# A decoder kernel on one core: a third seven-product unit pair in the early parts of both down projections, and two in the last part

## The chip, the core and the metric

The kernel runs on one core of one Trainium2 chip. Times are microseconds (us) of that core on the device. A kernel's time is the median of several runs; its profile is of one execution by itself. In profile rows PE is TensorE (PEld its weight loads), DVE is VectorE, ACT is ScalarE, POOL is GpSimd, SP is SyncE, which issues the weight loads.

## The reference

Two decoder layers over 256 tokens of width 2048. The first layer mixes tokens with gated linear attention, the second with attention that has a forget gate; both also attend with 4 heads into 256 memory tokens, and the heads' outputs go through one output projection (`wo`). Behind each mixer stands the feed-forward network that the change is about:

```python
def conv_ffn(h, w_up, conv_w, conv_b, w_down):
    u = causal_dwconv(h @ w_up, conv_w, conv_b)     # width 3, 2 x 5632 columns
    a, val = split_cols(u, [FFN_HIDDEN, FFN_HIDDEN])
    return (jax.nn.silu(a) * val) @ w_down          # 5632 -> 2048

# per layer
    x = x + mixer(...)
    h = rmsnorm(x, norm_ffn[i])
    x = x + conv_ffn(h, ffn_w_up[i], ffn_conv_w[i], ffn_conv_b[i], ffn_w_down[i])
# at the end
    return rmsnorm(x, norm_final)
```

Everything is float32 in and out.

## The kernel before

**Products.** TensorE's fast 32-bit type keeps fewer bits than float32, so each operand is held as a high part and a low part (the rounded value and the rest), and a product is three matmuls: high x high, low x high, high x low. Activations lie as chunks of 128 features (`A0`, `A1`, ... and `B0`, ...), each with its two parts for 256 tokens, made by `split` (ScalarE the high part, L464; VectorE the low part, L465).

**Units.** A weight panel is 512 output columns. It comes in units of two chunks (128 x 1024 values, 512 KB). SP loads a unit as `raw` (4 buffers), ScalarE rounds it to `whi` (L207), VectorE subtracts to `wlo` (L216); 3 buffers each. A unit gives 12 matmuls of 128x512: two chunks, two halves of the tokens, three products. Sums build up in PSUM tiles `acc` (4 banks). `proj_tm` does one panel, `proj_two` two panels at once with the last `late` units of both held back.

**Seven products.** `proj_seven` does two panels at once. For a pair of units (same chunks, panels f and f+1) that stands in `forms`, it takes the four blocks (two chunks, two panels) against two token halves as a 2x2 by 2x2 block product with 7 block products rather than 8: 21 matmuls, not 24. VectorE makes weight sums `t13` and `t24` (four 128x512 operations, L335 to L338), ScalarE and VectorE the high and low parts of raw unit 0, of half of raw unit 1 (`vhi`, `vlo`), of `t13` and of `t24`; the activations need sums too (`summed`: four `sf` operations of 128x128, then the parts of `forms`, 128x512). Four block products go to banks of their own (`ps_t`, `ps_s` twice, `ps_o`) and are added to `x` by `more` (s16, s167).

**Feed-forward network.** The hidden width is 44 chunks in three parts of 16, 16 and 12. For each part the "up" panels are computed, scaled, transposed through DRAM, and two chunks at a time go through `taken` (convolution, Silu, multiply, `split`), which is put behind a number of units by `later` and `passed`. Then the part's down projection adds its four panels f = 0 to 3 to `x`. Parts 0 and 1 have 8 units per panel; both panel pairs use `proj_seven` with unit pairs u = 3 and 5 (`SEVEN`). The last part has 6 units per panel: panels 0 and 1 by `proj_two`, 2 and 3 by `proj_tm`. In the last part of layer 1 the final norm's gain `gf` (1 MB) is loaded, and each panel is multiplied by it.

**Order.** A scheduler puts each engine's instructions in a fixed order, by priority (`tc.high_priority`; weights get `AHEAD`); an engine runs its instructions in that order.

Of the kernel before, what the change touches and what calls it, by code (L numbers as in the profile page):

```python
# [136 lines left out]
def _trunk(ctx: ExitStack, tc: tile.TileContext, xt, xtok, memt, wp, wgu, gns, gfin, cnv, par, msk, out):  # L137
# [128 lines left out]
                    for b in range(2):  # L266
                        evacs[i](b, acc[i][b][:, : units[i][0][2]])

    def proj_seven(keys, src, forms, evacs, pool, more):

        units = [where[k] for k in keys]
        count = len(units[0])
        base = min(min(u[1]) for u in units[0])
        acc = [[pacc.tile([P, 512], F32, name="acc", tag="acc") for _ in range(2)] for _ in keys]
        m1, m5, m6, m7 = (work(t, n) for t, n in (("t", 1), ("s", 2), ("o", 1), ("s", 2)))
        begun, calls = set(), {}

        def form(a, x, hi, lo, c):
            s = slice(c * 512, (c + 1) * 512)
            out = []  # L280
            for xs, w in ((x[0], hi), (x[1], hi), (x[0], lo)):
                out.append((a, xs, w[:, s]))
            return out

        def emit(groups):
            todo = [g[n] for n in range(2) for g in groups] + [g[2] for g in groups]
            for a, x, w in todo:
                k = id(a)
                calls[k] -= 1
                TE.matmul(a, x, w, start=k not in begun, stop=calls[k] == 0)  # L290
# [12 lines left out]
        def token(kc, b):  # L303
            return [src[kc - base][:, i, b * P : (b + 1) * P] for i in range(2)]

        def halves(raw, w):
            if w == NUNIT:
                hi, lo = (wpool.tile([P, w], F32R, name=n, tag=n, bufs=3) for n in ("whi", "wlo"))
            else:
                hi, lo = (pool.tile([P, w], F32R, name=n, tag=n) for n in ("vhi", "vlo"))  # L310
            casts.append(S.activation(hi, raw, AF.Copy))
            V.tensor_tensor(lo, raw, hi.bitcast(F32), ALU.subtract)
            return hi, lo

        def load(unit):
            off, kcs, n = unit
            raw = wpool.tile([P, NUNIT], F32, name="raw", tag="raw", bufs=4)
            loads.append(nc.sync.dma_start(raw, wp[off : off + P * NUNIT].rearrange("(p n) -> p n", p=P)))
            return raw

        for u in range(count):
            k0, k1 = units[0][u][1]
            if u not in forms:
                for i in range(2):
                    hi, lo = split_unit(units[i][u])
                    emit([form(acc[i][b], token(kc, b), hi, lo, c) for b in range(2) for c, kc in enumerate((k0, k1))])
                    if u == count - 1:
                        for b in range(2):
                            evacs[i](b, acc[i][b])
                continue  # L330
            s = forms[u]
            with tc.high_priority(offset=AHEAD + 40):
                r0, r1 = (load(units[i][u]) for i in range(2))
                t13, t24 = (pool.tile([P, 2, 512], F32, name=n, tag=n) for n in ("t13", "t24"))
                V.tensor_tensor(t13[:, 0, :], r1[:, :512], r0[:, :512], ALU.subtract)  # L335
                V.tensor_tensor(t13[:, 1, :], r1[:, 512:], r1[:, :512], ALU.subtract)
                V.tensor_tensor(t24[:, 0, :], r1[:, 512:], t13[:, 0, :], ALU.subtract)
# [614 lines left out]
    def add_seven(key, src, forms, pool):  # L952
        for f in (0, 2):
            def more(m1, m5, m6, m7, x0=x[f], x1=x[f + 1]):
                u, w = (pool.tile([P, 512], F32, name=n, tag=n) for n in ("s16", "s167"))
                V.tensor_tensor(x0[:, 0, :], x0[:, 0, :], m1, ALU.add)
                S.activation(u, m1, AF.Copy)
                V.tensor_tensor(u, u, m6, ALU.add)
                V.tensor_tensor(x1[:, 0, :], x1[:, 0, :], u, ALU.add)
                V.tensor_tensor(w, u, m7, ALU.add)  # L960
                V.tensor_tensor(x0[:, 1, :], x0[:, 1, :], w, ALU.add)
                V.tensor_tensor(x1[:, 1, :], x1[:, 1, :], w, ALU.add)
                V.tensor_tensor(x1, x1, m5.unsqueeze(1).to_broadcast([P, 2, 512]), ALU.add)

            proj_seven([(*key, g) for g in (f, f + 1)], src, forms, [add_panel(g) for g in (f, f + 1)], pool, more)

    def ffn(l, nx, h, m, then, ending=None):
        with tc.tile_pool(name=f"ffn{l}", bufs=1) as fp, ExitStack() as ends:
            sums = ends.enter_context(ExitStack())
            sp = sums.enter_context(tc.tile_pool(name=f"sums{l}", bufs=1))  # L970
            cw = fp.tile([P, 4 * 88], F32, name="cw")
# [2 lines left out]
            for u in us:  # L974
                nc.gpsimd.memset(u[:, :, :2], 0.0)
            turn = [0]
            forms = {u: sp.tile([P, 2, 4, P], F32R, name=f"forms{u}") for u in SEVEN}
            held = []

            def form(t):  # L980
                return lambda i: [t[:, h, i, :] for h in range(2)]

            def taken(j, base, u, i):
# [11 lines left out]
                S.activation(cv[0], cv[0], AF.Silu)  # L995
                V.tensor_tensor(cv[1], cv[0], cv[1], ALU.mult)
                split(m, j + i - base, cv[1])
                if base < PARTS[-1][0] and (j - base) // 2 in forms:
                    held.append(cv[1])
                    if i:  # L1000
                        summed(forms[(j - base) // 2])

            def summed(form):
                h0, h1 = (natural(h) for h in held)
# [24 lines left out]

                return evac  # L1030

            spare = None
            for p, (lo, hi) in enumerate(PARTS):
                if p == len(PARTS) - 1:
                    sums.close()
                    if ending is not None:
                        then, spare = ending(ends)
                js = list(range(lo, hi, 2))
                if not p:
                    proj_two([("up", l, j) for j in js[:2]], h, [panel(js[0], lo), panel(js[1], lo, 2)], 2)  # L1040
                    js = js[2:]
                for j in js:
                    proj_tm(("up", l, j), h, panel(j, lo))
                if p < len(PARTS) - 1:
# [35 lines left out]

    fin = StreamNorm()

    def ending(ends):
        op = ends.enter_context(tc.tile_pool(name="store", bufs=1))
        gf = op.tile([P, D], F32, name="gf")
        nc.sync.dma_start(gf, gfin.to_broadcast([P, D]))
        y = op.tile([P, 2, 512], F32, name="y")
        junk = op.tile([P, 1], F32, name="junk")

        def then(f, b):  # L1090
            fin.add(f, b)
            if f == 0 and b == 0:
                S.activation(junk, fin.sums[:, 0, 0:1], AF.Sqrt)
            dst = y if f == 3 else x[f]
            V.tensor_tensor(dst[:, b, :], x[f][:, b, :], gf[:, f * 512 : (f + 1) * 512], ALU.mult)
            if f < 3:
# [17 lines left out]
        return then, op  # L1114

    ffn(1, n, bufA, bufB, None, ending)


def _constants():
# [82 lines left out]
```

## Time and profile before

| | us |
|---|---|
| median of 3 runs | 2247.64 |
| lowest and highest run | 2246.07, 2249.72 |
| the profiled execution | 2246.29 |
| its span | 2244.5 |
| PE busy in it | 2230.9 (99%) |
| DVE busy in it | 1636.5 (73%) |
| ACT busy in it | 1310.9 (58%) |

Starts are counted from the beginning of the span. In a row of the timeline stand start, duration, engine, line, operation, output and inputs, shape and count, and in brackets the idle time of the engine before it with what ended it. Line numbers are those of the kernel before.

### The profile page before, as it was taken

Reading aid. Unit: us, or ns where it says so; the run is one execution under the profiler, and the core shown is the slowest. Engines: PE = TensorE matmul, PEld = TensorE weight load, DVE = VectorE, ACT = ScalarE, POOL = GpSimd, SP = SyncE. Lnnn points to the kernel's source line nnn. Section 1 sums busy time; section 2 is a strip of 40 time slices with the busy share of each in tenths; the row PEclk is TensorE's granted clock in tenths of the full one; section 3 lists DMA queues with packets and bytes.
Section 4 is the critical chain, followed back from the end, with each engine's and each line's share of the span. In section 5 each row is a group of like instructions: output and inputs, shape, how many; then the busy total and the mean of one; then the engine's idle time right before and its main releaser. Section 6 shows DMA issues by size and latency. Waiting matters only on the chain.

```text
span 2244.5 us, 29477 instructions
## 1 busy us (share of the span) xinstructions
PE 2230.9 (99%) x10288; PEld 1865.2 (83%) x10288; DVE 1636.5 (73%) x2509; ACT 1310.9 (58%) x1898; POOL 2.9 (0%) x15
## 2 busy tenths in 40 slices
PE   9999999999999999999999999999999999999998
PEld 7888888888888888888888988888888888888886
DVE  7568988667788677876776556766778867786766
ACT  7555666656564566545665555555666456654654
POOL 0000000000000000000000000000000000000000
PEclk9999999999999999999999999999999999999999
DMA  8875667677876778667777886677776677767774
GB/s 320 278 235 189 203 205 223 200 237 241 257 224 207 231 231 253 211 203 246 235 253 252 249 270 204 180 231 234 247 249 221 202 237 242 239 194 249 238 243 150
DMA packets 303772, 516.96 MB, mean 230 GB/s; under 512 B 178556, under 2 KB 187272, under 8 KB 303496
## 3 DMA queue, kind: packets, MB, share of 16 engines
q1 hardware_dynamic: 124296, 427.24, 58.5%
q10 hardware_dynamic: 179328, 87.85, 13.9%
q8 instruction: 80, 1.31, 0.2%
q14 instruction: 68, 0.56, 0.1%
HBM read 470.44 MB, written 44.58 MB: 229 GB/s over the span
## 4 chain that ended last, share of the span: by engine, by line
PE 97%; DMA 1%; DVE 1%; issue 0%; ACT 0%; SPq 0%; ACTq 0%; DVEq 0%
PE acc L228 26%; PE acc L229 26%; PE acc L232 26%; PE acc L290 13%; PE ps_s L290 1%; PE ps_o L290 0%; PE ps_t L290 0%; DMA raw<-wp 0%; DMA cb<-cdram 0%; PE ps_s L770 0%; PE ps_s L571 0%; PE ps_t L564 0%; PE ps_o L582 0%; DVE wlo L216 0%; PE ps_s L912 0%
## 5 line engine op out<-in xcount | busy, mean ns | idle before, releaser
L216 DVE TENSOR_TENSOR wlo<-raw,whi 128x1024 fp32r<-128x1024 f32 (+4 forms) x777 | 929.3, 1200 | 505.3 <-ACT whi L207 458.3
L207 ACT ACTIVATE whi<-raw 128x1024 fp32r<-128x1024 f32 (+4 forms) x777 | 808.0, 1042 | 745.2 <-PE acc L229 489.5
L228 PE MATMUL acc<-whi,B 128*128 128x512 f32 (+3 forms) x1536 | 586.2, 383 | 0.4 <-ACT whi L207 0.4
L229 PE MATMUL acc<-whi,B 128*128 128x512 f32 (+3 forms) x1536 | 584.8, 382 | 0.0
L228 PE MATMUL acc<-whi,A 128*128 128x512 f32 x1184 | 462.4, 392 | 1.5 <-ACT A L464 1.0
L229 PE MATMUL acc<-whi,A 128*128 128x512 f32 x1184 | 460.0, 390 | 0.0
L232 PE MATMUL acc<-wlo,B 128*128 128x512 f32 (+3 forms) x1536 | 401.0, 381 | 0.3 <-DVE wlo L216 0.3
L228 PEld LDWEIGHTS acc<-whi,B 128*128 128x128 f32 x1536 | 288.2, 188 | 51.1 <-ACT whi L207 0.7
L229 PEld LDWEIGHTS acc<-whi,B 128*128 128x128 f32 x1536 | 288.0, 188 | 49.6
L232 PEld LDWEIGHTS acc<-wlo,B 128*128 128x128 f32 x1536 | 285.5, 188 | 50.4 <-DVE wlo L216 0.6
L232 PE MATMUL acc<-wlo,A 128*128 128x512 f32 x1184 | 318.8, 390 | 0.3 <-DVE wlo L216 0.3
L228 PEld LDWEIGHTS acc<-whi,A 128*128 128x128 f32 x1184 | 222.3, 188 | 49.9 <-ACT A L464 1.6
L232 PEld LDWEIGHTS acc<-wlo,A 128*128 128x128 f32 x1184 | 222.0, 188 | 46.7 <-DVE wlo L216 0.7
L229 PEld LDWEIGHTS acc<-whi,A 128*128 128x128 f32 x1184 | 222.6, 188 | 45.9 <-DVE A L468 0.2
L991 ACT ACTIVATE cv<-u,cw 128x256 f32<-128x256 f32 x176 | 97.3, 589 | 25.6 <-DMA u<-turned 25.3
L290 PE MATMUL acc<-whi,B 128*128 128x512 f32 x416 | 108.3, 390 | 0.0
L290 PE MATMUL acc<-whi,A 128*128 128x512 f32 x416 | 108.2, 390 | 0.0
L290 PEld LDWEIGHTS acc<-whi,B 128*128 128x128 f32 x416 | 78.0, 188 | 16.7 <-ACT whi L207 0.3
L290 PEld LDWEIGHTS acc<-whi,A 128*128 128x128 f32 x416 | 78.1, 188 | 16.6
L992 DVE SCALAR_TENSOR_TENSOR cv<-u,cw,cv 128x256 f32<-128x256 f32 x176 | 78.7, 479 | 16.3 <-ACT cv L991 16.2
L384 DVE STREAM_TRANSPOSE square<-scaled 128x512 f32<-128x512 f32 x122 | 79.9, 690 | 0.0
L993 DVE SCALAR_TENSOR_TENSOR cv<-u,cw,cv 128x256 f32<-128x256 f32 x176 | 77.3, 477 | 0.0
(231 smaller groups left out, 1572.9 us busy)
## 6 DMA issues: line engine op xcount, KB each, us to landing
raw<-wp SPq DMA_DIRECT2D x743, 512.0 KB, 4.3
turned<-square ACTq DMA_DIRECT2D x61, 512.0 KB, 4.4
u<-turned ACTq DMA_DIRECT2D x176, 128.0 KB, 5.1
raw<-wp SPq DMA_DIRECT2D x32, 384.0 KB, 3.3
raw<-wp SPq DMA_DIRECT2D x24, 388.0 KB, 4.9
back<-xturned ACTq DMA_DIRECT2D x64, 128.0 KB, 5.6
xturned<-square ACTq DMA_DIRECT2D x12, 512.0 KB, 4.1
back<-turned ACTq DMA_DIRECT2D x32, 128.0 KB, 4.2
```

The costliest lines, as they stand in the source:

```text
L207: casts.append(S.activation(hi[:, s], raw[:, s], AF.Copy))
L216: V.tensor_tensor(lo[:, s], raw[:, s], hi[:, s].bitcast(F32), ALU.subtract)
L228: TE.matmul(acc[:, :n], xh, hi[:, s], start=first and j == 0, stop=False)
L229: TE.matmul(acc[:, :n], xl, hi[:, s], start=False, stop=False)
L232: TE.matmul(a, xh, ls, start=False, stop=stop)
L290: TE.matmul(a, x, w, start=k not in begun, stop=calls[k] == 0)
L384: V.transpose(self.square[:, :, :, b], src.rearrange("p (c t) -> p c t", t=32))
L991: S.activation(r, v[:, 2:], AF.Identity, bias=w[3], scale=w[2])
L992: V.scalar_tensor_tensor(r, v[:, 1 : T + 1], w[1], r, ALU.mult, ALU.add)
L993: V.scalar_tensor_tensor(r, v[:, :T], w[0], r, ALU.mult, ALU.add)
```

## The change

Four things change. (1) `SEVEN` has a list for each panel pair: panels 0 and 1 keep u = 3 and 5, panels 2 and 3 of parts 0 and 1 also get u = 7, the last unit. (2) Panels 0 and 1 of the last part go through `proj_seven` with u = 2 and 4; with `early`, `more` is emitted right behind u = 4, ahead of the last unit. The space of the sums (`sums`) is kept until that pair is emitted. (3) The ending is split: `gf` is loaded at the start of the second network, the rest made in the last part as before; `s16` and `s167` lie in the buffers `scaled`. (4) Memory heads 1 to 3 of layer 0 get a priority of 64.

```diff
-SEVEN = (3, 5)
+SEVEN = ((3, 5), (3, 5, 7))
+LAST = (2, 4)
...
-    def proj_seven(keys, src, forms, evacs, pool, more):
+    def proj_seven(keys, src, forms, evacs, pool, more, early=False):
...
                     if u == count - 1:
                         for b in range(2):
                             evacs[i](b, acc[i][b])
+                if u == count - 2 and count - 1 in forms:
+                    evacs[1](1, acc[1][1])
                 continue
...
             emit([form(m6, s(1), *v3, 0), form(acc[0][1], token(k1, 1), *v3, 1)])
-        more(m1, m5, m6, m7)
+            if u == count - 1:
+                for i, b in ((0, 0), (1, 0), (0, 1)):
+                    evacs[i](b, acc[i][b])
+            if early and u == max(forms):
+                more(m1, m5, m6, m7)
+
+        if not early:
+            more(m1, m5, m6, m7)
...
     def mem_attention(pool, l, q, hd, dst):
+        with tc.high_priority(offset=0 if l or not hd else 64):
+            mem_head(pool, l, q, hd, dst)
+
+    def mem_head(pool, l, q, hd, dst):
...
-                u, w = (pool.tile([P, 512], F32, name=n, tag=n) for n in ("s16", "s167"))
+            u, w = (tp.tile([P, 512], F32, name=n, tag="scaled", bufs=2) for n in ("s16", "s167"))
...
+            if ending:
+                then = ending[0](ends)
...
-            forms = {u: sp.tile([P, 2, 4, P], F32R, name=f"forms{u}") for u in SEVEN}
+            tiles = [sp.tile([P, 2, 4, P], F32R, name=f"forms{i}") for i in range(3)]
...
-            spare = None
+            parts = {lo: dict(zip(SEVEN[1] if p < len(PARTS) - 1 else LAST, tiles)) for p, (lo, _) in enumerate(PARTS)}
             for p, (lo, hi) in enumerate(PARTS):
-                if p == len(PARTS) - 1:
-                    sums.close()
-                    if ending is not None:
-                        then, spare = ending(ends)
...
                 if p < len(PARTS) - 1:
-                    add_seven(("down", l, p), m, {u: form(t) for u, t in forms.items()}, sp)
+                    for f, at in zip((0, 2), SEVEN):
+                        add_seven(key, f, m, {u: form(forms[u]) for u in at}, sp)
                     continue
-                add_out(("down", l, p), m, then, spare)
+                if LAST:
+                    add_seven(key, 0, m, {u: form(forms[u]) for u in LAST}, sp, then)
+                sums.close()
+                spare = ending[1](ends) if ending else None
...
+                for f in range(2, 4):
+                    proj_tm((*key, f), m, add_panel(f, then), spare if f == 3 else None)
...
-    def ending(ends):
+    def opened(ends):
...
+    def closing(ends):
+        op = ends.enter_context(tc.tile_pool(name="store", bufs=1))
+        made["y"] = op.tile([P, 2, 512], F32, name="y")
+        return op
-    ffn(1, n, bufA, bufB, None, ending)
+    ffn(1, n, bufA, bufB, None, (opened, closing))
```

The order of instructions shows where the last part's low parts stand. VectorE, layer 0, around the low parts of hidden chunks 10 and 11 (`A10`, `A11`, the last two); before:

```order
L216 TENSOR_TENSOR wlo_10151<-raw_10147,whi_10148 128x1024
L992 SCALAR_TENSOR_TENSOR cv0_10153<-u1_4580,cw_4577,cv0_10153 128x256
L992 SCALAR_TENSOR_TENSOR cv1_10157<-u1_4580,cw_4577,cv1_10157 128x256
L996 TENSOR_TENSOR cv1_10127<-cv0_10123,cv1_10127 128x256
L993 SCALAR_TENSOR_TENSOR cv0_10153<-u1_4580,cw_4577,cv0_10153 128x256
L993 SCALAR_TENSOR_TENSOR cv1_10157<-u1_4580,cw_4577,cv1_10157 128x256
L216 TENSOR_TENSOR wlo_10181<-raw_10177,whi_10178 128x1024
L465 TENSOR_TENSOR A10_94<-cv1_10127,A10_94 128x128x2
L996 TENSOR_TENSOR cv1_10157<-cv0_10153,cv1_10157 128x256
L216 TENSOR_TENSOR wlo_10199<-raw_10195,whi_10196 128x1024
L465 TENSOR_TENSOR A11_95<-cv1_10157,A11_95 128x128x2
```

The same place now (`wlo_10252` and `wlo_10262` belong to the second seven-product pair, `wlo_10285` and `wlo_10317` to the last units of the two panels, `wlo_10352` to the first unit of panel 2; `ps_t` holds the first of the seven products):

```order
L313 TENSOR_TENSOR wlo_10252<-t13_10216,whi_10251 128x1024
L313 TENSOR_TENSOR wlo_10262<-t24_10217,whi_10261 128x1024
L1014 TENSOR_TENSOR cv1_10192<-cv0_10188,cv1_10192 128x256
L1014 TENSOR_TENSOR cv1_10234<-cv0_10230,cv1_10234 128x256
L971 TENSOR_TENSOR x0_80<-x0_80,ps_t_10017 128x512
L217 TENSOR_TENSOR wlo_10285<-raw_10281,whi_10282 128x1024
L217 TENSOR_TENSOR wlo_10317<-raw_10313,whi_10314 128x1024
L217 TENSOR_TENSOR wlo_10352<-raw_10348,whi_10349 128x1024
L475 TENSOR_TENSOR A10_94<-cv1_10192,A10_94 128x128x2
L475 TENSOR_TENSOR A11_95<-cv1_10234,A11_95 128x128x2
```

The two low parts now stand behind the low parts of both last units and of the next panel's first unit, and behind the add of `ps_t`; before, each stood right behind one weight.

TensorE, the same stage, where chunk 10 is first used; before:

```order
L232 MATMUL acc_9973<-wlo_10181,A9_93 128x512
L228 MATMUL acc_9970<-whi_10196,A10_94 128x512
L229 MATMUL acc_9970<-whi_10196,A10_94 128x512
L228 MATMUL acc_9970<-whi_10196,A11_95 128x512
L228 MATMUL acc_9971<-whi_10196,A10_94 128x512
```

L229 multiplies the low part. Now, from the last product into `ps_t` to the first of the last units:

```order
L291 MATMUL ps_t_10017<-wlo_10223,A8_92 128x512
L291 MATMUL acc_10013<-wlo_10223,A9_93 128x512
L291 MATMUL ps_s_10018<-wlo_10252,forms1_4584 128x512
L291 MATMUL ps_s_10020<-wlo_10252,forms1_4584 128x512
L291 MATMUL ps_o_10019<-wlo_10262,forms1_4584 128x512
L291 MATMUL acc_10014<-wlo_10262,A9_93 128x512
L291 MATMUL acc_10013<-whi_10282,A10_94 128x512
L291 MATMUL acc_10014<-whi_10282,A10_94 128x512
L291 MATMUL acc_10015<-whi_10314,A10_94 128x512
L291 MATMUL acc_10016<-whi_10314,A10_94 128x512
L291 MATMUL acc_10013<-whi_10282,A11_95 128x512
L291 MATMUL acc_10014<-whi_10282,A11_95 128x512
```

Eight products with the high parts of chunks 10 and 11 (two more follow these six with chunk 11) come first, then the low part of chunk 10; the last product into `ps_t` stands 14 matmuls ahead of that. In the whole program 128x512 matmuls go from 8888 to 8864.

TensorE at the output projection of layer 0, around the last memory head's output (`ps_o`), which becomes chunk `A15`; before:

```order
L229 MATMUL acc_3740<-whi_4184,A14_98 128x512
L582 MATMUL ps_o_4098<-pts_4096,mv0_132 128x256 x2
L228 MATMUL acc_3737<-whi_4134,A15_99 128x512
```

and now:

```order
L229 MATMUL acc_3738<-whi_4134,A14_98 128x512
L596 MATMUL ps_o_4098<-pts_4096,mv0_132 128x256 x2
L230 MATMUL acc_3737<-whi_4134,A14_98 128x512
L230 MATMUL acc_3738<-whi_4134,A14_98 128x512
L229 MATMUL acc_3739<-whi_4184,A14_98 128x512
L230 MATMUL acc_3739<-whi_4184,A14_98 128x512
L229 MATMUL acc_3740<-whi_4184,A14_98 128x512
L230 MATMUL acc_3740<-whi_4184,A14_98 128x512
L229 MATMUL acc_3737<-whi_4134,A15_99 128x512
```

Six matmuls with `A14` now stand between the head's output and the first use of `A15`.

More of the change, by code (lines that the diff above doesn't have):

```diff
@@ L950, in add_out, with add_seven, more @@
             proj_tm((*key, f), src, add_panel(f, then), spare if f == 3 else None)
-    def add_seven(key, src, forms, pool):
-        for f in (0, 2):
-            def more(m1, m5, m6, m7, x0=x[f], x1=x[f + 1]):
-                u, w = (pool.tile([P, 512], F32, name=n, tag=n) for n in ("s16", "s167"))
[L956 to L965, printed above, removed]
+    def add_seven(key, f, src, forms, pool, then=None):
+        x0, x1 = x[f], x[f + 1]
+        def more(m1, m5, m6, m7):
+            u, w = (tp.tile([P, 512], F32, name=n, tag="scaled", bufs=2) for n in ("s16", "s167"))
+            V.tensor_tensor(x0[:, 0, :], x0[:, 0, :], m1, ALU.add)
+            S.activation(u, m1, AF.Copy)
+            V.tensor_tensor(u, u, m6, ALU.add)
+            V.tensor_tensor(x1[:, 0, :], x1[:, 0, :], u, ALU.add)
+            V.tensor_tensor(w, u, m7, ALU.add)
+            V.tensor_tensor(x0[:, 1, :], x0[:, 1, :], w, ALU.add)
+            V.tensor_tensor(x1[:, 1, :], x1[:, 1, :], w, ALU.add)
+            V.tensor_tensor(x1, x1, m5.unsqueeze(1).to_broadcast([P, 2, 512]), ALU.add)
+        proj_seven([(*key, g) for g in (f, f + 1)], src, forms, [add_panel(g, then) for g in (f, f + 1)], pool, more,
+                   then is not None)
     def ffn(l, nx, h, m, then, ending=None):
         with tc.tile_pool(name=f"ffn{l}", bufs=1) as fp, ExitStack() as ends:
+            if ending:
+                then = ending[0](ends)
             sums = ends.enter_context(ExitStack())
@@ L997, in taken @@
                 split(m, j + i - base, cv[1])
-                if base < PARTS[-1][0] and (j - base) // 2 in forms:
+                if (j - base) // 2 in parts[base]:
                     held.append(cv[1])
                     if i:
-                        summed(forms[(j - base) // 2])
+                        summed(parts[base][(j - base) // 2])
             def summed(form):
@@ L1043, in ffn @@
                     proj_tm(("up", l, j), h, panel(j, lo))
+                key = ("down", l, p)
                 if p < len(PARTS) - 1:
-                    add_seven(("down", l, p), m, {u: form(t) for u, t in forms.items()}, sp)
+                    for f, at in zip((0, 2), SEVEN):
+                        add_seven(key, f, m, {u: form(forms[u]) for u in at}, sp)
                     continue
-                add_out(("down", l, p), m, then, spare)
+                if LAST:
+                    add_seven(key, 0, m, {u: form(forms[u]) for u in LAST}, sp, then)
+                sums.close()
+                spare = ending[1](ends) if ending else None
+                if not LAST:
+                    proj_two([(*key, f) for f in range(2)], m, [add_panel(f, then) for f in range(2)], 1)
+                for f in range(2, 4):
+                    proj_tm((*key, f), m, add_panel(f, then), spare if f == 3 else None)
     def preparing(name, dst):
@@ L1081, in _trunk @@
     fin = StreamNorm()
-    def ending(ends):
-        op = ends.enter_context(tc.tile_pool(name="store", bufs=1))
+    made = {}
+    def opened(ends):
+        op = ends.enter_context(tc.tile_pool(name="gain", bufs=1))
         gf = op.tile([P, D], F32, name="gf")
         nc.sync.dma_start(gf, gfin.to_broadcast([P, D]))
-        y = op.tile([P, 2, 512], F32, name="y")
         junk = op.tile([P, 1], F32, name="junk")
@@ L1093, in then @@
                 S.activation(junk, fin.sums[:, 0, 0:1], AF.Sqrt)
+            y = made.get("y")
             dst = y if f == 3 else x[f]
@@ L1112, in then @@
                 (nc.scalar if g == 1 else nc.sync).dma_start(out[b, :, g * 512 : (g + 1) * 512], t)
-        return then, op
-    ffn(1, n, bufA, bufB, None, ending)
+        return then
+    def closing(ends):
[3 more added lines that the diff above has]
+    ffn(1, n, bufA, bufB, None, (opened, closing))
 def _constants():
```

1 line of the change is left out of this document (added).

## The prediction

> **What bounds the kernel now.** The page comes first: busy shares and the chain that ended last.
>
> ```profile
> PE 2230.9 (99%) x10288; PEld 1865.2 (83%) x10288; DVE 1636.5 (73%) x2509; ACT 1310.9 (58%) x1898; POOL 2.9 (0%) x15
> PE 97%; DMA 1%; DVE 1%; issue 0%; ACT 0%; SPq 0%; ACTq 0%; DVEq 0%
> ```
>
> TensorE (PE) is busy throughout and its matmuls are 97% of the chain, so removed matmuls can be worth their full time, and a wait put ahead of a matmul costs its full length. What one is worth, the chain in order of time tells, in a row with 72 of them in succession; the two windows below give one seven-product stage (both panel pairs, and its second pair alone) and the first pair of the last part of layer 0.
>
> ```profile
> 643.51 16.32 PE acc L290 x72
> 643.00:728.00 85.00, 85.00 (x375) 69.98 (x374) 70.85 (x88) 46.17 (x53) 0.00 (x0) 1.00 0.63 209
> 685.00:728.00 43.00, 43.00 (x191) 35.44 (x190) 35.67 (x41) 21.20 (x22) 0.00 (x0) 1.00 0.59 201
> 1117.00:1143.00 26.00, 26.00 (x117) 21.52 (x116) 18.38 (x27) 15.83 (x21) 0.31 (x1) 1.00 0.72 235
> ```
>
> 16.32 / 72 = 0.2267 us per matmul of 128x512. The columns of a window are its length and the busy time of PE, weight load, VectorE (DVE), ScalarE (ACT), POOL; then the clock, 1.00 here, and the DMA share. Where seven-product pairs stand, DVE is at 70.85 / 85 = 83%; in the last part it has 7.6 of 26 us free.
>
> How long a DVE operation keeps the next one off is read from starts in the DVE timeline (start, duration, operation, count), since two operations overlap by about 0.08 us.
>
> ```profile
> 1112.56 1.22 DVE L216 TENSOR_TENSOR wlo<-raw,whi 128x1024 fp32r<-128x1024 f32 x1
> 1113.69 0.87 DVE L992 SCALAR_TENSOR_TENSOR cv<-u,cw,cv 128x256 f32<-128x256 f32 x2
> 1114.48 0.42 DVE L996 TENSOR_TENSOR cv<-cv,cv 128x256 f32<-128x256 f32 x1
> 1114.82 0.88 DVE L993 SCALAR_TENSOR_TENSOR cv<-u,cw,cv 128x256 f32<-128x256 f32 x2
> ...
> 1116.75 0.64 DVE L465 TENSOR_TENSOR A<-cv,A 128x256 fp32r<-128x256 f32 x1
> 1117.21 0.43 DVE L996 TENSOR_TENSOR cv<-cv,cv 128x256 f32<-128x256 f32 x1
> ...
> 1119.18 1.30 DVE L384 STREAM_TRANSPOSE square<-scaled 128x512 f32<-128x512 f32 x2
> 1120.40 0.60 DVE L465 TENSOR_TENSOR A<-cv,A 128x256 fp32r<-128x256 f32 x1
> ```
>
> So a weight's low part (`wlo`) takes 1.13, a convolution step 0.79 / 2 = 0.395, a gate multiply 0.34, the low part of a hidden chunk (`A<-cv,A`) 0.46, two transposes 1.22. From a seven-product pair, and the groups:
>
> ```profile
> 655.14 0.69 DVE L312 TENSOR_TENSOR vlo<-raw,vhi 128x512 fp32r<-128x512 f32 x1
> 655.74 0.68 DVE L337 TENSOR_TENSOR t<-raw,t 128x512 f32<-128x512 f32 x1
> ...
> L1007 DVE TENSOR_TENSOR sf<-cv,cv 128x128 f32<-128x128 f32 x8 | 2.3, 284 | 0.0
> ```
>
> A 512-wide add takes 0.60, one of the sums of activations (`sf`) 0.284 - 0.08 = 0.20.
>
> **Matmuls removed.** A seven-product pair is 21 matmuls instead of 24. Eight pairs of units change (one in each of four early stages, two in each last part): 24 matmuls x 0.2267 = 5.44 us off. All of them are on the path. This is 0.24% of the time; what a measurement of this kernel can tell from no change is about 0.2%, so the change can hardly show unless nothing is paid back.
>
> **Third pair, u = 7, in the four early stages (panels 2 and 3).** DVE gets three low parts and five 512-wide operations in place of two low parts: 3 x 1.13 + 5 x 0.60 - 2 x 1.13 = 4.1 us. In the window 685 to 728 DVE has 35.67 us of work in 43.0; afterwards 35.7 + 4.1 = 39.8 in 43.0 - 0.7 = 42.3. That cover of 2.5 us hides it, so I cost the stage at nothing but short waits: 0 to 0.5 each, 0.1 taken, 0.4 in all. The sums for u = 7 are made in the panels 0 and 1 before it, four `sf` and one 512-wide operation more there, 4 x 0.20 + 0.60 = 1.4 us, against these waits of DVE for others in that pair:
>
> ```profile
> 679.70 1.22 DVE L216 TENSOR_TENSOR wlo<-raw,whi 128x1024 fp32r<-128x1024 f32 x1 [0.91 <-ACT whi L207]
> 681.97 1.22 DVE L216 TENSOR_TENSOR wlo<-raw,whi 128x1024 fp32r<-128x1024 f32 x1 [1.04 <-PE acc L290]
> ```
>
> They hold 0.91 + 1.04 = 1.95 us. If the cover is gone, PE pays what is over (second rival).
>
> **First pair of each last part: here the sum is decided.** Call T0 the first matmul of that projection, and compare when the low part of hidden chunk 10 is made and when it is used:
>
> ```profile
> 1117.60 0.39 PE L228 MATMUL acc<-whi,A 128*128 128x512 f32 x1
> ...
> 1138.51 0.64 DVE L465 TENSOR_TENSOR A<-cv,A 128x256 fp32r<-128x256 f32 x1
> ```
>
> Before, it is made at 1138.51 + 0.64 = 1139.15, 21.5 us after T0, and used after 121 matmuls, 27.4 after T0: 5.9 us to spare. DVE's first low part of that stage starts at 1112.56, so the next operation, at 1113.69, is 3.91 us ahead of T0. In the changed order there stand from that point up to and with chunk 10's low part: 14 low parts of weights x 1.13 = 15.8; 12 operations of 512 (eight of the weight sums, two `vlo`, the low part of `forms1`, `x0<-x0,ps_t`) x 0.60 = 7.2; 12 convolution steps x 0.395 = 4.7; 4 multiplies x 0.34 = 1.4; two transposes 1.2; 3 low parts of chunks x 0.46 = 1.4; 4 `sf` x 0.20 = 0.8. Together 32.5: ready 32.5 - 3.9 = 28.6 after T0 if DVE never waits. It will. The first weight sum waits for its raw weights, as these did:
>
> ```profile
> DVE t L335 <- DMA raw<-wp: 9.8, 12, 1.6
> ```
>
> That is 9.8 / 12 = 0.8 us a time, and there are two per last part: 1.6, and 0.3 for a weight buffer that PE still holds. So 28.6 + 1.9 = 30.5. PE wants chunk 10's low part after 122 matmuls (2 x 24 + 21 + 24 + 21 + 8), 122 x 0.2267 = 27.66 after T0. PE then stands 30.5 - 27.66, **2.9 us per layer**, with nothing behind it to do: the whole last unit uses chunks 10 and 11.
>
> A bound from below, without DVE's load: on DVE `x0<-x0,ps_t` and three weight low parts now stand ahead of chunk 10's low part. `ps_t` is finished by the 109th matmul, which starts 108 x 0.2267 = 24.5 after T0 and takes 0.39: 24.9. Then 0.60 + 3 x 1.13 + 0.64 = 4.6 gives 29.5, a stall of 1.9. From above: both raw waits at the longest, 1.6 each in place of 0.8, give 4.4 or so. So 1.9 to 4.4, and 2.9 is taken as the sum of the rows themselves. What is queued behind on DVE: chunk 11's low part, the sums `s16`, `s167` and the next panel's low parts; PE's next panel stands later by the same stall, so they are not late a second time.
>
> **Gain vector, moved.** Its 1 MB load goes from the last part to the start of the second feed-forward network, onto the weights' queue (SP), where it waits for the last attention head's output, near 1472.
>
> ```profile
> L1086 SPq DMA_DIRECT2D gf<-gfin x1: 328/328/328, 2045.8 to 2045.8; - x1
> DMA to landing us min/median/max: 7.6/7.6/7.6
> 1470.00:1480.00 10.00, 10.00 (x47) 8.33 (x46) 7.36 (x10) 6.19 (x16) 0.00 (x0) 1.00 0.39 117
> ```
>
> It took 7.6 us to land; between 1470 and 1480 the DMA engines are 39% busy. The weight loads behind it on SP can be up to some us later, and they run ahead by several units: 0 to 1 us, 0.2 taken, as the free 61% of that window could take it.
>
> **Memory heads of layer 0, earlier.** PE waits here for the last heads' outputs:
>
> ```profile
> 418.35 1.18 PE L228 MATMUL acc<-whi,A 128*128 128x512 f32 x4 [0.28 <-ACT A L464]
> ...
> 422.01 1.18 PE L228 MATMUL acc<-whi,A 128*128 128x512 f32 x4 [0.70 <-ACT A L464]
> ```
>
> 0.28 + 0.70 = 1.0 at stake; in the order the last head's output now stands some six matmuls (6 x 0.2267 = 1.4 us) ahead of its use. Gain 0 to 1.0; half taken, 0.5, since the softmax ahead of it is not shortened. The other edits (where `s16` and `s167` lie, the later release of the sums' space) have no row of their own and only touch space: 0, inside the bounds above.
>
> **Sum.** -5.44 - 0.5 + 2 x 2.9 + 0.4 + 0.2 = +0.46 us. The profiled execution took 2246.29, 1.35 below the median 2247.64. So 2246.75 for it, and 2248.1 as a median: no change that can be told.
>
> **The rivals.**
> 1. *No stall*: DVE gets ahead during the up-projection before T0 and chunk 10 comes in time. For: 7.6 us are free in the window 1117 to 1143. Against: the lower bound of 1.9 doesn't depend on DVE's lead. -5.44 - 0.5 + 0.2 gives 2240.55, median **2241.9**. Chance 0.12.
> 2. *VectorE becomes the bound of every seven-product stretch* (the slower side): waits of each kind add, since low parts have only three buffers and wait for PE, and PE for them. In an early stage three waits for raw weights at 0.8 to 1.6 (the row above) are 2.4 to 4.8, less the free 2.5 that is 0 to 2.3, 1.5 taken. Four stages at 1.5 and two last parts at 4.4 are 14.8: -5.44 - 0.5 + 0.2 + 14.8 = +9.1, median **2256.7**. It decides once waits come to over 10 us. For: DVE would be at 39.8 / 42.3 = 94% there. Against: 2.5 us stay free. Chance 0.16.
> 3. *DVE's operations don't overlap*, so durations, not starts, add: 14 x 1.22 + 12 x 0.69 + 12 x 0.435 + 4 x 0.42 + 1.30 + 3 x 0.64 + 4 x 0.284 = 36.6 in place of 32.5, a stall of 7.0 per layer, **2256.3**. Against: 1112.56 + 1.22 is 1113.78, and the next started at 1113.69. The Trainium skill, "VectorE: DVE Perf Modes", section "The DRAIN you can't avoid", says that the next operation doesn't start until the pipe has emptied; the trace shows a start 0.09 us before the end, so the trace decides. Chance 0.03.
> 4. *A stall slows the clock.* At the kernel's end PE stands, and the granted clock falls:
>
> ```profile
> 2230.00:2245.00 15.00, 5.08 (x22) 3.75 (x20) 7.54 (x24) 3.85 (x12) 0.00 (x0) 0.81 0.43 140
> ```
>
> There 0.19 of 15 us, 2.85 us, is missing; as much behind each stall would give 2248.1 + 5.7 = **2253.8**. Against: that window has 10 us without PE, the stall is 3. The Trainium skill, "TensorE: Matmul & The Clock Gate", section "Part 1: The HAM clock gate (the "warmup" mystery)", has the clock halve after an idle window of about 3.4 us; no run here shows a stall of that length amid work. Chance 0.04.
>
> **How the numbers follow.** Forecast 0.65, all of it within 0.2% (2243.1 to 2252.1); faster 0.12 is the first rival; slower 0.16 + 0.03 + 0.04 = 0.23. The forecast's own range: -5.44 - 1.0 + 3.8 = -2.6, 2245.0; up to -5.44 + 8.8 + 2.0 + 1.0 = +6.4, 2254.0. Stretched towards both sides, 2243.5 to 2255.0 leaves out the first rival and about half of the second and third.
>
> **What would show it.** PE 24 matmuls of 128x512 fewer. In each last part's first pair a wait of PE of 2 to 4 us for VectorE's `A<-cv,A` (`B<-cv,B` in layer 1), just ahead of the last unit, and hardly any elsewhere; chunk 10's low part about 30 us after T0. I am wrong if that wait is under 1 us (the order's cost is hidden), if the four early stages show waits over 0.5 us each, or if the granted clock falls below 1.00 behind the stall.

## The result and the profile after

| | before | changed |
|---|---|---|
| median of 15 runs, us | 2246.97 | 2250.46 |
| lowest and highest run | 2245.63, 2249.72 | 2247.91, 2255.11 |
| the profiled execution | 2246.29 | 2250.13 |
| its span | 2244.5 | 2248.3 |

The ratio is 1.0019, interval 1.0012 to 1.0025: 0.2% slower, with an interval that leaves out no change, where 2248.1 was forecast. 24 matmuls went, 5.4 us; that was paid back and 3.5 us more. The page of the changed kernel, busy times:

```profile
PE 2228.8 (99%) x10264; PEld 1859.1 (83%) x10264; DVE 1686.6 (75%) x2611; ACT 1327.1 (59%) x1924; POOL 2.9 (0%) x15
```

PE has 24 instructions fewer (10288 before), VectorE (DVE) 50 us more work. The waits of PE in the changed kernel (us in total, times, longest):

```profile
PE acc L229 <- ACT whi L208: 1.8, 3, 1.2
PE ps_o L174 <- DVE B L171: 1.4, 1, 1.4
PE acc L291 <- DVE B L475: 1.4, 1, 1.4
PE acc L291 <- DVE A L475: 1.4, 1, 1.4
PE acc L291 <- ACT A L474: 1.0, 1, 1.0
PE acc L291 <- ACT B L474: 1.0, 1, 1.0
PE ps_o L291 <- DVE wlo L313: 0.8, 2, 0.4
PE ps_s L291 <- DVE wlo L313: 0.4, 1, 0.4
```

The second row stood there before as well (`ps_o L173`). The third to sixth are new: the low part and the high part of a hidden chunk, once in each layer. Where they stand, the timeline of PE shows, layer 0's last part from its first matmul (T0) to the first one of panel 2:

```profile
1115.31 1.98 PE L291 MATMUL acc<-whi,A 128*128 128x512 f32 x8
...
1141.63 0.50 PE L291 MATMUL ps_o<-wlo,forms 128*128 128x512 f32 x1 [0.40 <-DVE wlo L313]
...
1143.33 2.10 PE L291 MATMUL acc<-whi,A 128*128 128x512 f32 x8 [0.96 <-ACT A L474]
1146.82 1.66 PE L291 MATMUL acc<-whi,A 128*128 128x512 f32 x6 [1.39 <-DVE A L475]
...
1150.58 0.39 PE L229 MATMUL acc<-whi,A 128*128 128x512 f32 x1
```

138 matmuls at 0.2267 are 31.3 us; they took 1150.58 - 1115.31 = 35.3: 4.0 us of waits. In layer 1:

```profile
2170.13 1.98 PE L291 MATMUL acc<-whi,B 128*128 128x512 f32 x8
...
2202.14 1.65 PE L291 MATMUL acc<-whi,B 128*128 128x512 f32 x6 [1.42 <-DVE B L475]
...
2205.92 0.39 PE L229 MATMUL acc<-whi,B 128*128 128x512 f32 x1
```

35.8, so 4.5. The two last parts pay back 8.5 us for 2.7 us of matmuls (12 of them). VectorE over the same stretch of layer 0:

```profile
1110.00 0.49 DVE L1010 SCALAR_TENSOR_TENSOR cv<-u,cw,cv 128x256 f32<-128x256 f32 x1 [0.85 <-ACT cv L1009]
...
1111.19 1.22 DVE L217 TENSOR_TENSOR wlo<-raw,whi 128x1024 fp32r<-128x1024 f32 x1
1112.33 0.88 DVE L1010 SCALAR_TENSOR_TENSOR cv<-u,cw,cv 128x256 f32<-128x256 f32 x2
...
1129.62 0.69 DVE L338 TENSOR_TENSOR t<-raw 128x512 f32<-128x512 f32 x1 [1.49 <-DMA raw<-wp]
...
1141.49 0.75 DVE L1014 TENSOR_TENSOR cv<-cv,cv 128x256 f32<-128x256 f32 x2
1142.17 0.68 DVE L971 TENSOR_TENSOR x<-x,ps_t 128x512 f32<-128x512 f32 x1
1142.76 3.49 DVE L217 TENSOR_TENSOR wlo<-raw,whi 128x1024 fp32r<-128x1024 f32 x3
1146.17 1.06 DVE L475 TENSOR_TENSOR A<-cv,A 128x256 fp32r<-128x256 f32 x2
```

From 1112.33 VectorE works, with one gap of 1.49 us for raw weights, until chunk 10's low part lets PE go at 1146.82: 34.5 us. The multiply that chunk 10 needs was done near 1141.9; what follows it, an add and three weight low parts, 1146.17 - 1142.17 = 4.0 us, is not needed by PE as early. One of the four early stages, the first of layer 0, by the window of its second panel pair:

```profile
685.00:728.00 43.00, 43.00 (x190) 35.30 (x189) 39.63 (x49) 21.89 (x23) 0.00 (x0) 1.00 0.57 188
```

VectorE is at 39.63 of 43 us, and PE hasn't stood: the third pair was hidden there.

### The profile page after: what moved, and what is told of

Its sections match the earlier page's. It is cut to its first block, busy times and chain, and to the rows that moved or that the text cites. A ratio compares the mean times of both kernels' runs of the same rounds, so it can differ in the third digit from the quotient of the medians.

```text
span 2248.3 us, 29571 instructions
## 1 busy us (share of the span) xinstructions
PE 2228.8 (99%) x10264; PEld 1859.1 (83%) x10264; DVE 1686.6 (75%) x2611; ACT 1327.1 (59%) x1924; POOL 2.9 (0%) x15
## 5 line engine op out<-in xcount | busy, mean ns | idle before, releaser
L217 DVE TENSOR_TENSOR wlo<-raw,whi 128x1024 fp32r<-128x1024 f32 (+4 forms) x761 | 909.9, 1199 | 447.5 <-ACT whi L208 413.8
L208 ACT ACTIVATE whi<-raw 128x1024 fp32r<-128x1024 f32 (+4 forms) x761 | 791.1, 1041 | 692.8 <-PE acc L230 461.1
L229 PE MATMUL acc<-whi,B 128*128 128x512 f32 (+3 forms) x1488 | 567.5, 383 | 0.0
L230 PE MATMUL acc<-whi,B 128*128 128x512 f32 (+3 forms) x1488 | 566.4, 382 | 0.0
L229 PE MATMUL acc<-whi,A 128*128 128x512 f32 x1136 | 444.3, 393 | 1.9 <-ACT whi L208 1.8
L230 PE MATMUL acc<-whi,A 128*128 128x512 f32 x1136 | 442.7, 391 | 0.0
L233 PE MATMUL acc<-wlo,B 128*128 128x512 f32 (+3 forms) x1488 | 388.0, 381 | 0.0
L229 PEld LDWEIGHTS acc<-whi,B 128*128 128x128 f32 x1488 | 279.2, 188 | 48.5
L233 PE MATMUL acc<-wlo,A 128*128 128x512 f32 x1136 | 305.9, 390 | 0.3 <-DVE wlo L217 0.3
L229 PEld LDWEIGHTS acc<-whi,A 128*128 128x128 f32 x1136 | 213.2, 188 | 49.0 <-ACT whi L208 4.3
L230 PEld LDWEIGHTS acc<-whi,A 128*128 128x128 f32 x1136 | 213.2, 188 | 44.2 <-DVE A L478 0.3
L291 PE MATMUL acc<-whi,B 128*128 128x512 f32 x464 | 122.2, 391 | 2.7 <-DVE B L475 1.4
L291 PE MATMUL acc<-whi,A 128*128 128x512 f32 x464 | 122.1, 390 | 2.4 <-DVE A L475 1.4
L291 PEld LDWEIGHTS acc<-whi,A 128*128 128x128 f32 x464 | 86.9, 188 | 21.7 <-DVE A L475 1.8
L312 ACT ACTIVATE whi<-t 128x1024 fp32r<-128x1024 f32 x48 | 50.9, 1061 | 74.4 <-DVE t L341 42.4
L1010 DVE SCALAR_TENSOR_TENSOR cv<-u,cw,cv 128x256 f32<-128x256 f32 x176 | 78.5, 479 | 16.0 <-ACT cv L1009 15.8
```

The lines of the kernel that those rows point to most:

```text
L208: casts.append(S.activation(hi[:, s], raw[:, s], AF.Copy))
L217: V.tensor_tensor(lo[:, s], raw[:, s], hi[:, s].bitcast(F32), ALU.subtract)
L229: TE.matmul(acc[:, :n], xh, hi[:, s], start=first and j == 0, stop=False)
L230: TE.matmul(acc[:, :n], xl, hi[:, s], start=False, stop=False)
L233: TE.matmul(a, xh, ls, start=False, stop=stop)
L1010: V.scalar_tensor_tensor(r, v[:, 1 : T + 1], w[1], r, ALU.mult, ALU.add)
```

## The experiments

Times are medians of 7 to 11 runs, each against runs of the kernel before on the same chip (medians 2246.51, 2246.14 and 2247.05 in the three groups: e1 to e5, e6 to e9, e10 and e11).

| kernel | us | ratio to before, interval |
|---|---|---|
| e1, early parts alone | 2243.24 | 0.9988 (0.9979 to 0.9996) |
| e2, last parts alone | 2251.54 | 1.0021 (1.0012 to 1.0030) |
| e3, chunks first | 2252.10 | 1.0027 (1.0016 to 1.0038) |
| e5, heads back | 2249.74 | 1.0012 (1.0003 to 1.0021) |
| e6, panels first too | 2245.97 | 1.0000 (0.9991 to 1.0008) |
| e7, one pair in the last part | 2246.91 | 1.0003 (0.9994 to 1.0011) |
| e8, e1 with the gain late | 2242.87 | 0.9988 (0.9979 to 0.9997) |
| e9, neither | 2245.86 | 0.9998 (0.9990 to 1.0007) |
| e10, one pair, mended | 2241.62 | 0.9977 (0.9968 to 0.9986) |
| e11, two pairs, mended | 2248.08 | 1.0003 (0.9994 to 1.0012) |

**Which half costs: e1, e2, e9.**

```diff
-LAST = (2, 4)                    # e1, and e9
+LAST = ()
-SEVEN = ((3, 5), (3, 5, 7))      # e2, and e9
+SEVEN = ((3, 5), (3, 5))
```

> The changed kernel without the seven-product pairs of the last part (panels 0 and 1 of it go through proj_two as before); the third pair at u = 7 of the early parts, the moved gain load and the memory heads stay. Theory (the loss lies in the two last parts): 12 matmuls fewer than before, -2.7 us, waits in the early stages about +1.0 as in the trace of the changed kernel, heads -0.4, so about 2 us under the kernel before, 2244.9. Rival (VectorE's work at u = 7 is what costs): about +1 to +2 against before, 2248 to 2249.

> The changed kernel with u = 3 and 5 alone in the early parts, both pairs of the last part kept. Theory: 12 matmuls fewer, -2.7, the waits in the last parts as in the changed kernel, 3.7 + 4.3 = +8.0, the wait of 1.3 us near 1174 behind layer 0's last part with it, heads -0.4: 5 to 6.5 us over before, 2252 to 2253.5. Rival (the early stages cost): under +1.5, 2248.5 or less.

> The changed kernel with u = 3 and 5 alone in the early parts and no seven-product pair in the last part: what is left is the moved gain load, the memory heads' priority and where s16 and s167 lie. Theory: these come to -0.4 (heads) and 0 to +1 (gain): 2246 to 2247.5, and e1 against it is the price of the third pair alone, -2.7 + 0.5 to 1.0. Rival (the side edits brought what e1 gained): 2243 to 2244.5.

The theory held in all three; e1 gained more than the 2.1 us expected. Without the last part's pairs the change is a gain, 2243.24; with them alone it is a loss, 2251.54, with the same waits in the profile (0.9 to 1.0 and 1.4 us in each layer). e9 equals the kernel before, so the third early pair is what e1 gains: 2243.24 - 2246.51 = -3.3 with it, 2245.86 - 2246.14 = -0.3 without; 12 matmuls are 2.7.

**What the wait in the last part hangs on: e3.** `tc.issue_after` queues instructions behind another on its engine, with the same work.

```diff
+    hold[:] = [(None, last[1])] * 2 + [(last[0], last[1])]   # ahead of the last unit: last = chunk 11's high and low part
...
+    with behind(held):           # ScalarE: whi of panel 2's first unit behind chunk 11's high part
         casts.append(S.activation(hi[:, s], raw[:, s], AF.Copy))
...
+    with behind(h[1]):           # VectorE: three wlo behind chunk 11's low part
         V.tensor_tensor(lo[:, s], raw[:, s], hi[:, s].bitcast(F32), ALU.subtract)
...
+    with behind(last[1]):
         more(m1, m5, m6, m7)
```

> The changed kernel with the order mended: in the last part VectorE's low parts of the last units and of panel 2's first unit, and the adds of the four extra products, are queued behind the low part of chunk 11, and ScalarE's high part of panel 2's first unit behind the high part of chunk 11. The same work, in another order. Theory (place in the queue): the wait for chunk 10's low part, 1.6 us a layer, goes, the one for its high part shrinks from 1.1 to about 0.5, the waits for the weight low parts (0.6 to 1.2) stay, and the wait near 1174 goes: 5 to 6.5 us under the changed kernel, 2244 to 2245.5, below the kernel before. Rival (VectorE has too much work in that stage whatever the order): the waits move to the last units' low parts, no gain, 2250.

The wait for chunk 10's low part went, but the time didn't: 2252.10. PE in e3, at panel 2's first matmuls, and VectorE ahead of that:

```profile
1144.70 3.92 PE L298 MATMUL acc<-whi,A 128*128 128x512 f32 x16 [0.29 <-ACT A L484]
...
1156.95 0.50 PE L236 MATMUL acc<-whi,A 128*128 128x512 f32 x1 [2.13 <-DVE x L964]
```
```profile
1154.30 0.67 DVE L984 TENSOR_TENSOR s<-s,ps_s 128x512 f32<-128x512 f32 x1
1155.00 0.69 DVE L985 TENSOR_TENSOR x<-x,s 128x512 f32<-128x512 f32 x1
1155.61 0.68 DVE L986 TENSOR_TENSOR x<-x,s 128x512 f32<-128x512 f32 x1
1156.22 0.68 DVE L964 TENSOR_TENSOR x<-x,acc 128x512 f32<-128x512 f32 x1
```

The last unit now waits 0.29 us in this view. But panel 2's second sum needs a PSUM bank that L964 (`x<-x,acc`) empties, and that add stands behind four adds for the extra products (L983 to L986): 2.13 us here, and the same again in layer 1. The rival, a wait that only moves on, was right for this order.

**Is VectorE full, or only in the wrong order: e6.** The adds of the extra products are emitted behind the panels' adds, and the norm's sums behind both.

```diff
-            if early and u == max(forms):
-                with behind(last[1]):
-                    more(m1, m5, m6, m7)
...
+        more(m1, m5, m6, m7)
...
-    [add_panel(g, then) for g in (f, f + 1)]
+    [add_panel(g) for g in (f, f + 1)]          # then(g, b) at the end of more
```

> The order of e3, and the adds of the four extra products behind the adds of the panels, so that PSUM banks for panel 2 come free sooner (the norm's sums follow both). In e3 the wait ahead of the last unit went from 2.7 to 0.5 us a layer, and 2.3 us a layer came up new at panel 2's first matmul in the second bank, for the add x0<-x0,acc that stood behind s16 and s167. Theory (each wait is a place in VectorE's queue): that wait goes too, 4 to 4.6 us under e3, about 2247 to 2248, and about 3 under the changed kernel; what stays is 0.5 for chunk 10's high part and 0.6 to 1.2 for weight low parts. Rival (VectorE is full, any order only moves the wait on): again 2251 or more.

2245.97, 6 us under e3, more than the 4 to 4.6 expected, and equal to the kernel before. So some of it was order: the bank wait is gone. The profile is of an execution of 2248.97, 3.0 over the median; these waits stay in it:

```profile
PE ps_s L298 <- DVE wlo L320: 1.8, 2, 1.2
PE ps_o L298 <- DVE wlo L320: 0.8, 2, 0.4
```

The weight low parts of the second pair are late. Not only work stands ahead of them: in layer 0 VectorE had waited 3.04 us for raw weights, twice the 1.49 of the changed kernel. And behind PE's waits the granted clock falls, amid the work:

```profile
1131.37 0.69 DVE L347 TENSOR_TENSOR t<-raw 128x512 f32<-128x512 f32 x1 [3.04 <-DMA raw<-wp]
```
```profile
1143.84:1147.25 3.41, 3.24 (x9) 2.28 (x8) 3.02 (x5) 1.81 (x3) 0.31 (x1) 0.50 0.13 38
```

In that window of 3.41 us the clock (third figure from the end) is 0.50. From T0 to panel 2, 1115.34 to 1151.31, are 36.0 us for 138 matmuls, 4.7 over; half the clock for 3.41 us makes 1.7 of them.

**Less of it: e7, e10.**

```diff
-LAST = (2, 4)
+LAST = (2,)
```

> The changed kernel with one seven-product pair in the last part, at u = 2, instead of two; the rest as changed. It takes 4.1 + 1.4 us of VectorE's work (weight sums, low parts, sums of activations) from the stretch ahead of chunk 10's low part, which was 3.1 us late with both. Theory: the waits there go to under 1 us a layer; against the changed kernel 6 matmuls more, +1.4, and 6 to 8 us of waits fewer: 2243 to 2246. Rival (a single pair costs as much as it brings, since what is late is the adds of the extra products, which stay): 2248 to 2250.

2246.91, a little above what the theory gave. With one pair, `more` is emitted behind u = 2, and six of its adds now come ahead of chunk 11's multiply; PE waits for that chunk's high part, 1.7 us in each layer, where under 1 was expected. VectorE and PE in e7:

```profile
1143.14 0.68 DVE L976 TENSOR_TENSOR x<-x,s 128x512 f32<-128x512 f32 x1
1143.74 0.68 DVE L977 TENSOR_TENSOR x<-x,s 128x512 f32<-128x512 f32 x1
1144.35 1.22 DVE L217 TENSOR_TENSOR wlo<-raw,whi 128x1024 fp32r<-128x1024 f32 x1
1145.48 0.60 DVE L475 TENSOR_TENSOR A<-cv,A 128x256 fp32r<-128x256 f32 x1
```
```profile
PE acc L291 <- ACT A L474: 1.7, 1, 1.7
PE acc L291 <- ACT B L474: 1.7, 1, 1.7
```

e10 is e7 in the order of e6, and with the gain vector late as in e8.

> One seven-product pair (u = 2) in the last part, in the order of e6 (low parts of chunks 10 and 11 ahead of the last units' weights, the extra products' adds behind the panels' adds), and the gain vector late as in e8. In e7 PE waited 1.9 us a layer for chunk 11's high part, whose multiply stood behind five adds of the extra products and two weight low parts. Theory (place in the queue): without them ahead, that wait is under 0.4 us a layer; against e8 6 matmuls fewer, -1.36: 2241.5 to 2242.5, the fastest of all. Rival (two panels at once with seven products in the last part always cost what they bring): 2243.5 to 2246.

2241.62, within the 2241.5 to 2242.5 of the theory, 5.4 us under the kernel before, the fastest of all. The profile has no wait of PE between 1130 and 1160; VectorE waits for PE there:

```profile
1142.93 1.23 DVE L224 TENSOR_TENSOR wlo<-raw,whi 128x1024 fp32r<-128x1024 f32 x1 [1.13 <-ACT whi L213]
1145.82 0.69 DVE L959 TENSOR_TENSOR x<-x,acc 128x512 f32<-128x512 f32 x1 [1.67 <-PE acc L298]
```

It has 18 matmuls fewer, 4.1 us by the row of 72. That it beats e8 rests on 0.9977 against 0.9988, whose intervals overlap.

**The side edits: e5, e8, e11.**

```diff
-        with tc.high_priority(offset=0 if l or not hd else 64):      # e5
+        with tc.high_priority(offset=0):
...
-        nc.sync.dma_start(gf, gfin.to_broadcast([P, D]))             # e8, e10, e11
+        made["load"] = lambda: nc.sync.dma_start(gf, gfin.to_broadcast([P, D]))
...
+                if ending:                                           # at the last part
+                    with tc.issue_after(loads[-1].ins):
+                        made["load"]()
```

> The changed kernel with the memory heads of layer 0 at their old priority. Theory: waits of 0.86 and 0.44 come back at the output projection of layer 0, 0.4 us in all over the changed kernel, 2250.9, hardly to be told in the time, but in the trace between 395 and 425. Rival: the heads' work placed earlier costs elsewhere, and without it the time is the same or lower.

The theory fell. The last head's output stands at the same place among PE's matmuls without the priority, and the waits of 0.28 and 0.70 don't come back. What moved the head was something else in the change; which, wasn't tried.

> The kernel e1 (no seven-product pair in the last part) with the gain vector loaded at the last part of layer 1, as before the change, instead of at the second network's start. Theory: the early load costs 0 to 1.5 us in some executions (a wait of PE near 1494 of 0.9 to 1.5 stands in the profiles of e2, e3 and e5, none in those of e1 and of the changed kernel): 0 to 1 under e1, 2242.3 to 2243.3. Rival (the wait near 1494 is the transposes' own, or the late load collides in turn): the same as e1 or up to 1 over.

2242.87 against 2243.24, not to be told apart. The wait near 1494 that was asked about stands in the profiles of e2, e3, e5, e6, e7 and e9, all with the early load; in the changed kernel and e1, also with it, it is missing; and so it is in e8, e10 and e11, with the late one. In e2:

```profile
1493.65 0.50 PE L229 MATMUL acc<-whi,B 128*128 128x512 f32 x1 [0.89 <-ACT whi L208]
```

Six of eight with the early load, none of three without, about 1 us each: it points to the load, but by counts of single executions.

> e6 (two pairs in the last part, order mended) with the gain vector late. Theory: 0 to 1 us under e6, waits of 2.8 and 1.8 in the last parts stay, for weight low parts that VectorE makes late: 2245 to 2246, above e8 and e10, since the second pair costs VectorE 5.5 us it has no room for. Rival: with the gain load out of the way it falls below e8, under 2242.9.

2248.08 where 2245 to 2246 was expected, by the ratio the same as e6. Its profile has 3.1 us of waits for `whi` in layer 1's last part that e6 hasn't, 0.9 and 2.2; the longer one stands behind a raw unit that came late to ScalarE's `vhi`, ahead of the `whi` that PE wanted:

```profile
2185.22 0.63 ACT L319 ACTIVATE vhi<-raw 128x512 fp32r<-128x512 f32 x1 [2.74 <-DMA raw<-wp]
2185.76 1.04 ACT L213 ACTIVATE whi<-raw 128x1024 fp32r<-128x1024 f32 x1
```
```profile
2186.82:2190.23 3.41, 3.38 (x8) 2.71 (x9) 3.41 (x5) 3.41 (x6) 0.00 (x0) 0.50 0.20 49
```

Behind that wait the granted clock is 0.50 for 3.41 us, as in e6: 8 matmuls, 0.43 us each. Whether the late gain load had a part in the landing wasn't tried; e8 and e10 have the same load and no such wait. That the second pair isn't worth its VectorE time here agrees with theory; the size didn't.

## Why the prediction was right, and where its sum was short

The forecast was 2248.1, no change that can be told, by -5.44 of matmuls against two stalls of 2.9. The measured median was 2250.46, inside the 0.2% and the range; the mechanism, the place and the sign of each large term held, and the sum was 3.4 us short: +0.46 was forecast for the profiled execution, +3.84 came (2250.13 - 2246.29). That it was no further off is in part luck, since two terms below came out 0.8 and 1.2 us on the good side.

- **Matmuls, -5.44**: PE's count fell by 24, all of 128x512.
- **Last parts, 2 x 2.9 = +5.8, came as 8.5** (4.0 and 4.5). Two terms were taken too small, one in each layer. The sum put 32.5 of work and 1.9 of waits, 34.4, between the operation behind the first low part and PE's release by chunk 10, counted from a lead of 3.91. In layer 0 the stretch held, 1112.33 to 1146.82, 34.5, and the lead didn't: 1115.31 - 1112.33 = 2.98, since VectorE had stood 0.85 us for ScalarE's `cv` at 1110.00. That is 0.9 of the missing 1.1. In e2, where it doesn't stand there, the lead is 1115.70 - 1111.79 = 3.91 and PE goes on at 1146.30, 30.6 after T0 where 30.5 was forecast. In layer 1 the lead held and the waits didn't: 2170.13 - 2166.22 = 3.91, but from 2166.22 to 2202.14 are 35.9, 1.5 of the missing 1.6, with waits of 0.20, 0.52 and 1.99, 2.7 where 1.9 was taken:

```profile
2166.22 0.88 DVE L1010 SCALAR_TENSOR_TENSOR cv<-u,cw,cv 128x256 f32<-128x256 f32 x2
...
2184.95 0.69 DVE L338 TENSOR_TENSOR t<-raw 128x512 f32<-128x512 f32 x1 [1.99 <-DMA raw<-wp]
```

  Part of the wait came in other names than forecast: the high part on ScalarE (0.96) and the second pair's weights (0.40) come ahead of the low part (1.39), which by itself is under the 2 to 4 us that the prediction looked for. Only the whole stretch shows the price.
- **"So they are not late a second time": wrong.** The adds into `x0` and `x1` were late too, so the transposes through DRAM that make the next inputs were, and ScalarE, which issues the reads in its fixed order, stood until the transposed data had been written:

```profile
1168.41 4.06 ACTq L402 DMA_DIRECT2D back<-xturned  x4
1172.57 1.06 ACT L208 ACTIVATE whi<-raw 128x1024 fp32r<-128x1024 f32 x1 [4.77 <-PE acc L233]
```
```profile
1173.68 0.50 PE L229 MATMUL acc<-whi,A 128*128 128x512 f32 x1 [1.17 <-ACT whi L208]
```

  PE pays 1.2 us more there. The row names PE for ScalarE's 4.77 idle us, but the four DMA issues fill 4.06 of them. The profiles of e5, e6 and e11, with two pairs as well, have a wait of 0.8 to 1.2 in the same stretch; the kernel before, e1, e7, e8, e9 and e10 have none. That lateness is its cause is argued from order and times, not shown: e2 and e3, with two pairs, had none either, and the second of the two writes issued at L397 also took 7.8 us to land, where the slower of the two before took 4.2. In all PE's matmuls fell back there by 1.6 us against the profile before, from 0.3 later at panel 2's start (1150.58 and 1150.24) to 1.9 later near 1180.
- **Early stages, 0.4 in all, came as 1.6**: from the first matmul of a stage to the first behind it the four took 84.28, 84.28, 84.73 and 84.91 us, where they had taken 84.81, 84.81, 84.87 and 84.81. That is 1.1 less, for 2.7 of matmuls. About 1.0 of the 1.6 is what layer 1's two stages took beyond layer 0's, with waits of 0.1 and 0.3 for `whi`. Such waits come and go with the execution: e1 and e8, with the third pair, have none over 0.3, and e2 has 0.9 and twice 0.3 in a stage without it. That the work hides behind PE held.
- **Memory heads, -0.5, came as -1.3**: up to the wait for `back` the two profiles run alike (383.02 and 383.00), and the first seven-product stage starts at 642.07 where it had started at 643.35. The two waits, 0.28 and 0.70, are gone with what it took to get going again. But it isn't by the priority (e5).
- **Gain vector, 0.2**: nothing in this profile, perhaps 1 in others.

The terms give -5.44 + 8.5 + 1.6 + 1.6 - 1.3 = 5.0; two waits of the profile before near 1286 and 1292, 1.2 us in all by the gaps, are missing after, which leaves 3.8, as measured.

The rivals: the first, no stall, is out (4.0 and 4.5 us in the profile, and e2). The second, VectorE bound in every stretch, is out for the early stages (e1) and half right for the last part, where with two pairs even the better order keeps 1.0 to 1.6 us of waits for weight low parts a layer (e6), though VectorE itself waits for raw weights there. The third, no overlap of operations, would have taken 36.6 + 1.9 = 38.5 us for that stretch, which took 34.5. Here too the next operation starts before the one ahead ends (1111.19 + 1.22 = 1112.41, the next at 1112.33). The Trainium skill, "VectorE: DVE Perf Modes", section "The DRAIN you can't avoid", puts beside the rule that the prediction cites an exception: a next operation that is not held starts earlier. The starts in this trace are earlier.

The fourth, a clock that falls behind a stall, didn't come in the profiled execution: the longest wait was 1.4 us and both windows of the last parts show a granted clock of 1.00:

```profile
1116.00:1150.00 34.00, 31.25 (x134) 24.56 (x133) 32.45 (x50) 20.77 (x29) 0.31 (x1) 1.00 0.65 214
2171.00:2205.00 34.00, 30.82 (x131) 24.09 (x131) 31.41 (x48) 20.37 (x28) 0.00 (x0) 1.00 0.63 208
```

But it isn't out. In e6 and e11, with the same two pairs, the granted clock fell to 0.50 behind waits of 1.2 and 2.2 us. And a mean granted clock of 0.996 or 0.997 over the whole execution came in 5 of 15 executions of the changed kernel and in 6 of 51 of e2, e3, e5, e6 and e11, all with two pairs; in none of 55 of e1 and e7 to e10, nor in the 83 of the kernel before that ran beside the experiments, which all have 0.998 or 0.999. That points to such a stretch in some executions of the changed kernel, but no trace shows where it lay or what it cost there.

## What to carry to other kernels

Where one engine is saturated, price a saving on it by the helper's queue in the stretch in question: sum the helper's operations, start to start, from a point whose lead is known to the operand that is wanted, and take the lead and the helper's own waits with a margin, since 0.9 us of lead in one layer and 1.5 us of longer stretch in the other were a third to a half of the forecast stall. A stall that goes by reordering can come back one step later (e3: from the operand to the bank), so look at what else stands behind the same queue before counting it as gained. Half of a change can be the gain and half the loss: the third pair early and one pair in the last part, in an order that puts PE's next operand first, with the gain vector late, beat both the kernel before and the whole change.

## What the runs showed that was not expected

In layer 0 the stretch took 34.5 us by the trace against 34.4 by rows of the kernel before, but the close match is luck: the waits shown, 1.5, were 0.4 under those taken, and the rest, 33.0, was 0.5 over. In layer 1 the rest was 33.2. So the durations of VectorE's operations carry over to another mix of work within about 2%, and its waits don't.

A wait of 1.2 us with one of 0.4 behind it (e6), or one of 2.2 us (e11), was followed by 3.41 us at a granted clock of 0.50, amid work; in the changed kernel's profile waits of 0.4, 1.0 and 1.4 within 6 us were not. What decides it these runs don't show.

The changed kernel's runs spread over 7.2 us, those before over 4.1, and those of e10, from 2240.52 to 2246.01, over 5.5.
